# A trunk of four layers: the last down weights ahead of the embedding's, and the experts' outputs scattered as high and low parts

## Chip, cores and metric

The kernel runs on one core of a Trainium2 chip. The metric is the device time of one execution in microseconds, the median of several runs.

## What is computed

Two layers, each an attention and a channel mixer, on 256 tokens of width 1024, all in fp32. The change lies in the second layer's channel mixer, a mixture of experts that picks 2 of 8 for each token, and in the embedding behind it:

```python
def moe_swiglu(x, router_w, router_b, w_gate_up, w_down):
    ...
    for e in range(N_EXPERTS):
        y = y + combine[:, e:e + 1] * swiglu(xf, w_gate_up[e], w_down[e]).astype(F32)
...
    x = layer_norm(DEEPNORM_ALPHA * x + h, ln_ffn_g[i], ln_ffn_b[i])
    x = x + jax.nn.sigmoid(x @ ple_w_gate[i]) * (p[i] @ ple_w_proj[i])
```

An expert's weights are 3 x 1024 x 3584 numbers, 42 MiB; the eight together are 336 MiB.

## The kernel before

**The expert loop.** The experts are taken in turns 0 to 7 (`for e in range(NE)` in `experts`), each with room for 96 or 64 tokens: `GR` counts groups of 32 as (3, 2, 3, 3, 2, 3, 3, 2). `gather` picks an expert's tokens with a matrix of places `pm` (128 tokens x places, ones and zeros) and gives `xg`. An expert has four quarters q. `gate_up(e, q)` multiplies `xg` with gate and up weights, `trans(e, q)` turns the result `h` into `hT`, and `down(e, q)` adds its product with the down weights into `y`. The order in the program is gate_up(e, q), then down(e, q - 1), then trans(e, q); down(e, 3) comes after gate_up(e + 1, 0). Weights are fp32 and move through TensorE 256 columns at a time, four products side by side in strips of 32 columns of the array (`side_by_side`); the trace has two records of each fp32 product.

**The ring.** `ringtile` hands out tiles of 1 MiB in a fixed rotation of 22 (`TURNS`); a tile can be loaded once the one 22 places earlier has been used up. `fetch` takes the weights' tiles, one by one, in the order `items`, on the queue of SyncE; a tile of gate_up in q = 3 comes as two DMAs of 0.5 MiB, and so does the very last tile of down. The embedding's weights and the parts that are made of them take tiles of the same ring, so the order in which `ringtile` is called is also the order of the transfers.

**The scatter.** `y` of an expert stands in PSUM, 32 partitions for each quarter t of the 1024 outputs and 256 columns for each group g: two groups share one bank. `collect` copies it into the SBUF tile `ys`, t = 0, 1 on ACT and t = 2, 3 on DVE. `turn_back` transposes the places, `pm` to `pT`. A product `pT` x `ys` for each half n of the outputs and each block b of 128 tokens puts the rows back to their tokens, and `add` adds it with its gate to the residual `accx`. This hangs on the gate_up(e + 1, 1) of the next expert, as hooks behind its steps k = 0 (turn_back), 2 (first half) and 5 (second half): `SC`.

**The end.** `Finish` holds the second layer's embedding. In turn 7 at q = 3 `finish.load` and `finish.prepare` are called ahead of `down(7, 2)`. `load` brings the projection's weights (1 MiB) and the gate's (4 MiB); `prepare` splits them into an fp32r high part on ACT and the rest, the low part, on DVE (`split`), multiplies p with the projection (24 products), and loads the norm's vectors (1 MiB). `finish.end` is the tail, whose order on each engine is written by hand (`in_order`): collect, place products, adds with statistics, norm, turn into `xT`, products of x with the gate's parts, sigmoid, output. Outside of `in_order` the framework's scheduler fixes each engine's order when the kernel is built: as a rule the order of the program, with later work drawn ahead where it takes earlier work to be waiting.

Of the kernel before, what the change touches and what calls it, by code (L numbers as in the profile page):

```python
# [74 lines left out]
def trunk(ctx: ExitStack, tc: tile.TileContext, cst, x, p, ln_mix_g, ln_mix_b, ln_ffn_g, ln_ffn_b, ab_w_in,  # L75
# [45 lines left out]
    KT = 2  # L121
    SC = (0, 2, 5)
    NLAST = (256, 256)
# [5 lines left out]
    def mis():  # L129
        return psM.tile([P, 512], F32, tag="mis", name="mis")  # L130
# [302 lines left out]
    with pool("hl0", 5, side="right") as hl, ExitStack() as es0:  # L433
# [341 lines left out]
        moe = ctx.enter_context(pool("moe", 1, reuse_waits="tile"))  # L775
        lgT = moe.tile([64, P], F32, tag="pTe", name="lgT", bufs=1)
        V.memset(lgT, 0.0)
        V.memset(lgT[32:33, :], 1.0)
        pm_first = [moe.tile([P, 2 * 3 * CT], F32, tag="pm%d" % b, name="pm", bufs=2) for b in range(NB)]

# [107 lines left out]

    pt1 = moe.tile([P, D], F32, tag="ys", name="pt1", bufs=1)[:, :NB * 256].rearrange("p (b n) -> p b n", b=NB)
    nc.sync.dma_start(pt1, p[1, 0].rearrange("(b p) n -> p b n", p=P))  # L890
# [90 lines left out]
    def experts(rest, finish):  # L981
# [12 lines left out]
        items += [(NE - 1, 3, k) for k in range(chunks[3])]  # L994
        used, passed = [0], [None]

# [23 lines left out]
        def weights(*it):  # L1020
            assert items[used[0]] == it
            used[0] += 1
            return fetch(*it)

# [14 lines left out]
        def gather_first_turn():  # L1039

            xg = xgtile()
            moved = [A.copy(xg[:, k0:k0 + 4, :C0], first[k0 // 4][:, :4 * C0].rearrange("p (k t) -> p k t", t=C0))
                     for k0 in (0, 4)]
            st[0] = dict(xg=xg, pm=[t[:, :C0] for t in pm_first])
            return moved

        def gather(es, src):
# [4 lines left out]
            for b in range(NB):  # L1052
                t = moe.tile([P, 2 * 3 * CT], F32, tag="pm%d" % b, name="pm", bufs=2)
# [99 lines left out]

        def collect(y, ys, n):

            for g in range(n):
                for t in range(4):
                    (A.copy, V.tensor_copy)[t // 2](ys[CT * g:CT * (g + 1), 256 * t:256 * (t + 1)],
                                                    y[g // 2][CT * t:CT * (t + 1), 256 * (g % 2):256 * (g % 2 + 1)])

        def ystile():
            return moe.tile([P, D], F32, tag="ys", name="ys", bufs=1)

        def scatter(e):

            c_ = CT * gr[e]

            def turn_back(after):
                pT = st[e]["pT"] = moe.tile([P, NB, P], F32, tag="pTe", name="pTe", bufs=1)
                ps = mis()  # L1170
                with tc.issue_after(after.ins) if after else nullcontext():
                    for b in range(NB):
                        T.matmul(ps[:c_, b * P:(b + 1) * P], st[e]["pm"][b], ident, start=True, stop=True)
                A.copy(pT[:c_], ps[:c_, :S].rearrange("p (b t) -> p b t", b=NB))

            def half(n):
                def go(after):
                    if n == 0:
                        st[e]["ys"] = ystile()
                        collect(st[e]["y"], st[e]["ys"], gr[e])  # L1180
                    for b in range(NB):
                        po = mis()
                        with tc.issue_after(after.ins):
                            T.matmul(po, st[e]["pT"][:c_, b, :], st[e]["ys"][:c_, 512 * n:512 * (n + 1)],
                                     start=True, stop=True)
                        add(e, b, n, po)
                return go

            return turn_back, half(0), half(1)

# [10 lines left out]
        for e in range(NE):  # L1201
            for q in range(4):
# [16 lines left out]
                trans(e, q)  # L1219
                if e == NE - 1 and q == 3:  # L1220
                    scatter(e)[0](None)
        down(NE - 1, 3)
        ys = ystile()
        finish.end(functools.partial(collect, st[NE - 1]["y"], ys, gr[NE - 1]), ys, st[NE - 1]["pT"], CT * gr[NE - 1],
                   functools.partial(add, NE - 1))

# [6 lines left out]
    class Finish:  # L1233


        def load(self):
            self.pw, self.pTs = ringtile(), ringtile(F32R)
            nc.sync.dma_start(self.pw.rearrange("p (k n) -> p k n", n=D), ple_w_proj[1].rearrange("(k p) n -> p k n", p=P))
            w = ple_w_gate[1].rearrange("(k p) n -> p k n", p=P)
            self.raws = []  # L1240
            for n in range(2):
                for k0 in (0, 4):
                    self.raws.append(ringtile())
                    nc.sync.dma_start(self.raws[-1].rearrange("p (k n) -> p k n", n=512),
                                      w[:, k0:k0 + 4, 512 * n:512 * (n + 1)])

        def parts(self, t, src):
# [3 lines left out]

        def prepare(self):

# [5 lines left out]
            for b in range(NB):  # L1259
                for n in range(2):  # L1260
                    A.copy(self.pp[:, b, half[n]], p_part(([pTs[:, i] for i in range(NB)], pHL), b, n, mis()))
            self.HL = [[], []]
# [5 lines left out]
            self.gb = ringtile()  # L1268
            for i, v in enumerate((ln_ffn_g, ln_ffn_b)):
                nc.sync.dma_start(self.gb[:, D * i:D * (i + 1)], v[1:2, :].broadcast_to([P, D]))  # L1270
# [4 lines left out]
        def end(self, collect, ys, pT, c_, add):  # L1275
# [3 lines left out]
            pos, sgs, done = {}, [], {}  # L1279

            def place(b, n):
                pos[b, n] = acc()
                T.matmul(pos[b, n], pT[:c_, b, :], ys[:c_, half[n]], start=True, stop=True)

# [24 lines left out]
            with in_order():  # L1309
                collect()  # L1310
                for b in range(NB):
                    for n in range(2):
                        place(b, n)
# [69 lines left out]
```

## Time and profile before

| | |
|---|---|
| runs | 1373.24, 1374.14, 1376.18 us; median 1374.14 |
| profiled execution | 1376.53 us, of which the span from first to last instruction is 1374.8 |
| PE busy | 1345.0 us (98%) |
| DVE, ACT busy | 396.1 us (29%), 326.7 us (24%) |
| DMA | 433.77 MB, 316 GB/s over the span |
| expert loop | from 473 to 1331 us |

In what follows a time is counted from the span's first instruction. PE is TensorE, DVE is VectorE, ACT is ScalarE, SP is SyncE, which issues the DMAs. Matmuls are pipelined and the trace models their ends, so neighbouring groups overlap by 0.07 to 0.18 us.

### The profile page before, as it was taken

To read this page: it belongs to the slowest core of one execution; us is meant where nothing else is said; L and a number is where in the kernel's file an instruction comes from. 1 tells how busy PE (TensorE), PEld (TensorE's weight loads), DVE (VectorE), ACT (ScalarE), POOL (GpSimd) and SP (SyncE) were. 2 spreads that over 40 slices of the span, in tenths; PEclk is the share of its full clock that TensorE was granted. 3 is DMA by queue.
4 is the path that set the end of the run, shared out by engine and by line. 5 is a ranking of instruction groups with operands and counts; after the bars stand their busy time and mean duration, and the time that the engine had idled before them with its cause. 6 is when DMAs were issued, how large, how long until landed. Compare 5 with 4: busy or idle time off the path is not lost. (4 is left out here: it accounts for less than half of the span.)

```text
span 1374.8 us, 37450 instructions
## 1 busy us (share of the span) xinstructions
PE 1345.0 (98%) x16967; PEld 891.3 (65%) x16967; DVE 396.1 (29%) x781; ACT 326.7 (24%) x618; POOL 27.5 (2%) x31
## 2 busy tenths in 40 slices
PE   8999999999999999999999999999999999999977
PEld 6786788888776666655556555665555665665546
DVE  5466654555877700010010011001010002002054
ACT  4545444443557100110010010011010001001041
POOL 0000300000000000000000000000000000000000
PEclk9999999999999999999999999999999999999988
DMA  9462564566581899999999999999999999999950
GB/s 323 160 204 74 162 204 138 168 223 198 174 325 68 318 403 405 384 399 400 408 408 401 407 407 392 407 406 392 407 408 395 399 408 406 389 408 407 377 224 34
DMA packets 143146, 433.77 MB, mean 316 GB/s; under 512 B 8834, under 2 KB 14978, under 8 KB 142978
## 3 DMA queue, kind: packets, MB, share of 16 engines
q1 hardware_dynamic: 142834, 431.22, 82.4%
q8 instruction: 135, 2.21, 0.7%
q14 instruction: 33, 0.27, 0.1%
q10 hardware_dynamic: 144, 0.07, 0.0%
HBM read 430.21 MB, written 1.05 MB: 314 GB/s over the span
## 5 line engine op out<-in xcount | busy, mean ns | idle before, releaser
L90 PE MATMUL acc<-raw,xg 128*32 128x256 f32 x9408 | 519.7, 380 | 0.0
L90 PEld LDWEIGHTS acc<-raw,xg 128*32 128x32 f32 x9408 | 300.9, 110 | 209.7 <-issue 11.3
L90 PE MATMUL mis<-raw,hT 128*32 128x256 f32 x4704 | 262.7, 379 | 2.1 <-DMA raw<-in_moe_w_down 2.1
L90 PE MATMUL acc<-H,xT 128*128 128x512 f32 (+2 forms) x768 | 227.8, 380 | 0.8 <-ACT xT L90 0.8
L90 DVE TENSOR_TENSOR h<-h,acc 128x512 f32<-128x512 f32 (+2 forms) x64 | 37.8, 596 | 638.1 <-PE acc L90 478.9
L90 PEld LDWEIGHTS mis<-raw,hT 128*32 128x32 f32 x4704 | 151.8, 110 | 103.7 <-DMA raw<-in_moe_w_down 2.7
L90 DVE TENSOR_TENSOR L<-raw,H 128x1024 fp32r<-128x1024 f32 (+2 forms) x134 | 151.2, 1135 | 110.2 <-ACT H L90 109.6
L90 ACT CAST H<-raw 128x1024 fp32r<-128x1024 f32 (+2 forms) x138 | 133.6, 975 | 147.4 <-PE acc L90 136.9
L90 PEld LDWEIGHTS acc<-H,xT 128*128 128x128 f32 x768 | 141.1, 192 | 29.0 <-ACT xT L90 1.7
L90 ACT ACTIVATE h<-acc 128x512 f32<-128x512 f32 (+2 forms) x64 | 32.9, 522 | 482.8 <-PE acc L90 482.8
L90 PE MATMUL acc<-L,xT 128*128 128x512 f32 (+2 forms) x384 | 141.3, 374 | 0.0
L90 PEld LDWEIGHTS acc<-L,xT 128*128 128x128 f32 x384 | 72.6, 189 | 13.8 <-DVE L L90 1.2
L90 ACT COPY hT<-mis 128x512 f32<-128x512 f32 (+2 forms) x47 | 21.7, 495 | 196.2 <-PE mis L90 195.9
L90 PE MATMUL acc<-H,hT 128*128 128x512 f32 x176 | 55.8, 396 | 0.0
L90 DVE SCALAR_TENSOR_TENSOR x<-mis,gateT,x 128x512 f32<-128x512 f32 x28 | 21.0, 751 | 92.4 <-PE mis L90 90.9
L90 PE MATMUL acc<-H,oT 128*128 128x512 f32 x128 | 43.8, 410 | 0.0
L90 PEld LDWEIGHTS acc<-H,hT 128*128 128x128 f32 x176 | 33.0, 187 | 8.0
L90 PE MATMUL acc<-L,hT 128*128 128x512 f32 x88 | 34.8, 395 | 0.0
L90 DVE COPY ys<-mis 32x256 f32<-32x256 f32 x42 | 17.8, 423 | 48.7 <-ACT ys L90 41.5
L90 PEld LDWEIGHTS mis<-c,h 128*128 128x128 f32 (+1 forms) x212 | 21.7, 140 | 14.0 <-issue 12.3
L90 PE MATMUL mis<-c,h 128*128 128x128 f32 (+1 forms) x212 | 30.1, 271 | 0.0
L90 PEld LDWEIGHTS acc<-H,oT 128*128 128x128 f32 x128 | 23.9, 188 | 7.0 <-issue 1.9
(209 smaller groups left out, 783.7 us busy)
## 6 DMA issues: line engine op xcount, KB each, us to landing
raw<-in_moe_w_gate_up SPq DMA_DIRECT2D x192, 1024.0 KB, 18.2
raw<-in_moe_w_down SPq DMA_DIRECT2D x111, 1024.0 KB, 17.0
raw<-in_moe_w_gate_up SPq DMA_DIRECT2D x64, 512.0 KB, 12.8
raw<-in_ffn_w_gate_up SPq DMA_DIRECT2D x20, 1024.0 KB, 5.2
raw<-in_ffn_w_down SPq DMA_DIRECT2D x10, 1024.0 KB, 5.2
raw<-in_ab_w_in SPq DMA_DIRECT2D x9, 1024.0 KB, 7.7
raw<-in_ple_w_gate SPq DMA_DIRECT2D x8, 1024.0 KB, 13.3
raw<-in_ab_w_out SPq DMA_DIRECT2D x4, 1024.0 KB, 5.2
```

The source lines that it names most:

```text
L90: self.last = getattr(self.eng, name)(*args, **kw)
```

## The change

It has two parts.

**The scatter.** `turn_back` is called in `gather` (and for expert 0 in `gather_first_turn`), as soon as the places exist, so `pm` needs one buffer and `pT` three. `collect` now takes one half n of the outputs and splits each 32x256 piece of y into an fp32r high part (a copy on ACT) and a low part (a subtraction on DVE, which reads the high part). The high part has a buffer for each half, the low part one for both (`ysL0`). A place product becomes two fp32r products, high and low. The hooks move to k = 4 and k = 7.

**The end.** In turn 7 at q = 3 the projection's weights are loaded first, then all down weights that are left, and then the gate's weights and the norm's vectors. The projection is prepared behind `down(7, 2)`, and the splits of the gate's weights stand behind `down(7, 3)` in the program, directly ahead of `finish.end`. In `end` each half is collected and placed for both blocks before the next half.

```diff
-    SC = (0, 2, 5)
+    SC = (4, 7)
...
+        def turn_back(pm, n):
+            pT = moe.tile([P, NB, P], F32R, tag="pTe", name="pTe", bufs=3)
+            ps = mis()
+            for b in range(NB):
+                T.matmul(ps[:n, b * P:(b + 1) * P], pm[b], ident, start=True, stop=True)
+            A.copy(pT[:n], ps[:n, :S].rearrange("p (b t) -> p b t", b=NB))
+            return pT
...
         def gather(es, src):
...
-                st[e] = dict(xg=xg[i], pm=[t[:, o:o + ns[i]] for t in pm])
+                st[e] = dict(xg=xg[i], pT=turn_back([t[:, o:o + ns[i]] for t in pm], ns[i]))
...
+        def collect(y, c_, n):
+            ys = [moe.tile([P, 512], F32R, tag="ys" + "HL"[a] + str(n * (1 - a)), name="ys", bufs=1) for a in range(2)]
+            for g in range(c_ // CT):
+                for t in range(2):
+                    src = y[g // 2][CT * (2 * n + t):CT * (2 * n + t + 1), 256 * (g % 2):256 * (g % 2 + 1)]
+                    split(*(v[CT * g:CT * (g + 1), 256 * t:256 * (t + 1)] for v in ys), src)
+            return ys
...
             def half(n):
                 def go(after):
-                    if n == 0:
-                        st[e]["ys"] = ystile()
-                        collect(st[e]["y"], st[e]["ys"], gr[e])
+                    ys = collect(st[e]["y"], c_, n)
                     for b in range(NB):
                         po = mis()
                         with tc.issue_after(after.ins):
-                            T.matmul(po, st[e]["pT"][:c_, b, :], st[e]["ys"][:c_, 512 * n:512 * (n + 1)],
-                                     start=True, stop=True)
+                            for a in range(2):
+                                T.matmul(po, st[e]["pT"][:c_, b, :], ys[a][:c_], start=(a == 0), stop=(a == 1))
...
                 if e == NE - 1 and q == 3:
+                    finish.load_p()
+                    for it in items[used[0]:]:
+                        got[it] = fetch(*it)
                     finish.load()
-                    finish.prepare()
                 if q:
                     down(e, q - 1)
                 elif e:
                     down(e - 1, 3)
+                if e == NE - 1 and q == 3:
+                    finish.prepare_p()
...
         down(NE - 1, 3)
-        ys = ystile()
+        finish.prepare()
...
             with in_order():
-                collect()
-                for b in range(NB):
-                    for n in range(2):
+                for n in range(2):
+                    ys.append(collect(n))
+                    for b in range(NB):
                         place(b, n)
```

## Rows read from the trace of the kernel before

**Rows 1.** Stretches: span, busy per engine (count), clock, DMA share, GB/s

```profile
600.00:700.00 100.00, 99.09 (x1618) 57.76 (x1614) 8.93 (x16) 10.51 (x27) 2.70 (x4) 1.00 1.03 405
1200.00:1300.00 100.00, 100.00 (x1736) 58.34 (x1730) 8.65 (x15) 8.29 (x18) 0.00 (x0) 1.00 1.02 398
```

**Rows 2.** DMA queues, 640:1280 us in 40 slices: GB/s moved

```profile
GB/s 407 408 408 407 408 401 399 408 409 408 407 408 378 402 408 408 408 402 408 375 406 407 409 406 408 408 362 408 407 409 406 408 407 367 408 407 407 408 408 404
```

**Rows 3.** PE's waits, 600:1300: us in total, times, longest

```profile
PE mis L90 <- ACT xg L90: 0.9, 1, 0.9
```

**Rows 4.** DMA issues in 540:588, then 1010:1030: last column us to landing

```profile
raw<-in_moe_w_gate_up SPq DMA_DIRECT2D x11, 1024.0 KB, 6.7
...
raw<-in_moe_w_gate_up SPq DMA_DIRECT2D x6, 1024.0 KB, 18.6
```

**Rows 5.** Timeline of PE, the scatter of expert 6: start, us, work

```profile
1251.95 0.68 PE L90 MATMUL mis<-c,pm 128*96 128x128 f32 x4
1258.07 5.39 PE L90 MATMUL acc<-raw,xg 128*32 128x256 f32 x96
1263.38 1.98 PE L90 MATMUL mis<-ys,pTe 96*128 96x512 f32 x4
```

**Rows 6.** Last gate-up and last down issue: timeline, then us to landing

```profile
1286.26 0.71 SPq L830 DMA_DIRECT2D raw<-in_moe_w_gate_up  x1
raw<-in_moe_w_gate_up SPq DMA_DIRECT2D x1, 512.0 KB, 10.7
...
1317.73 0.34 SPq L830 DMA_DIRECT2D raw<-in_moe_w_down  x1
raw<-in_moe_w_down SPq DMA_DIRECT2D x1, 512.0 KB, 11.9
```

**Rows 7.** Timelines of PE, ACT and DVE, 1297:1332, some rows

```profile
1297.85 7.09 PE L90 MATMUL acc<-raw,xg 128*32 128x256 f32 x128
1319.35 1.93 PE L90 MATMUL mis<-raw,hT 128*32 128x256 f32 x32 [0.77 <-DMA raw<-in_moe_w_down]
1321.21 0.46 PE L90 MATMUL mis<-c,h 64*128 64x64 f32 x4
1327.19 3.66 PE L90 MATMUL mis<-raw,hT 128*32 128x256 f32 x64 [0.74 <-DMA raw<-in_moe_w_down]
...
1308.94 3.89 ACT L90 CAST raw<-raw 128x1024 fp32r<-128x1024 f32 x4
...
1310.65 8.03 DVE L90 TENSOR_TENSOR raw<-raw 128x1024 fp32r<-128x1024 f32 x7
```

**Rows 8.** Timelines of ACT, DVE and PE behind E

```profile
1330.91 0.74 ACT L90 COPY ys<-mis 32x256 f32<-32x256 f32 x2 [3.96 <-PE mis L90]
1332.57 0.74 ACT L90 COPY ys<-mis 32x256 f32<-32x256 f32 x2 [0.93 <-DVE ys L90]
...
1331.67 0.86 DVE L90 COPY ys<-mis 32x256 f32<-32x256 f32 x2 [12.99 <-ACT ys L90]
1335.47 0.75 DVE L90 SCALAR_TENSOR_TENSOR x<-acc,gateT,x 128x512 f32<-128x512 f32 x1 [1.27 <-PE acc L90]
1337.96 0.69 DVE L90 BATCH_NORM_STATS2 st<-x 128x6 f32<-128x512 f32 x1
...
1342.91 11.09 PE L90 MATMUL acc<-raw 128*128 128x512 f32 x40
1354.64 13.27 PE L90 MATMUL acc<-raw 128*128 128x512 f32 x80
```

**Rows 9.** Stretches of 5 us at the end, for the clock

```profile
1315.00:1320.00 5.00, 4.07 (x51) 2.22 (x53) 3.69 (x4) 2.60 (x4) 0.00 (x0) 1.00 0.94 355
1330.00:1335.00 5.00, 2.49 (x18) 1.14 (x11) 1.69 (x4) 1.45 (x4) 0.00 (x0) 0.79 0.01 3
1340.00:1345.00 5.00, 4.42 (x14) 3.27 (x14) 4.92 (x8) 1.18 (x2) 0.17 (x1) 0.50 0.00 0
1345.00:1350.00 5.00, 5.00 (x20) 4.00 (x20) 3.81 (x8) 0.00 (x0) 0.99 (x1) 0.84 0.00 2
```

More of the change, by code (lines that the diff above doesn't have):

```diff
@@ L775, in trunk @@
         moe = ctx.enter_context(pool("moe", 1, reuse_waits="tile"))
-        lgT = moe.tile([64, P], F32, tag="pTe", name="lgT", bufs=1)
+        lgT = moe.tile([64, P], F32, tag="pTe", name="lgT", bufs=3)
         V.memset(lgT, 0.0)
         V.memset(lgT[32:33, :], 1.0)
-        pm_first = [moe.tile([P, 2 * 3 * CT], F32, tag="pm%d" % b, name="pm", bufs=2) for b in range(NB)]
+        pm_first = [moe.tile([P, 2 * 3 * CT], F32, tag="pm%d" % b, name="pm", bufs=1) for b in range(NB)]
     ring = ctx.enter_context(pool("ring", 1, side="right", reuse_waits="tile"))
@@ L887, in trunk @@
         gather_first(b)
-    pt1 = moe.tile([P, D], F32, tag="ys", name="pt1", bufs=1)[:, :NB * 256].rearrange("p (b n) -> p b n", b=NB)
+    pt1 = moe.tile([P, 512], F32, tag="ysH0", name="pt1", bufs=1)[:, :NB * 256].rearrange("p (b n) -> p b n", b=NB)
     nc.sync.dma_start(pt1, p[1, 0].rearrange("(b p) n -> p b n", p=P))
@@ L1022, in weights @@
             used[0] += 1
-            return fetch(*it)
+            return got.pop(it) if it in got else fetch(*it)
         def place_of(dst, e, b, n):
@@ L1043, in gather_first_turn @@
                      for k0 in (0, 4)]
-            st[0] = dict(xg=xg, pm=[t[:, :C0] for t in pm_first])
+            st[0] = dict(xg=xg, pT=turn_back([t[:, :C0] for t in pm_first], C0))
             return moved
+        def turn_back(pm, n):
[5 more added lines that the diff above has]
+            return pT
         def gather(es, src):
@@ L1052, in gather @@
             for b in range(NB):
-                t = moe.tile([P, 2 * 3 * CT], F32, tag="pm%d" % b, name="pm", bufs=2)
+                t = moe.tile([P, 2 * 3 * CT], F32, tag="pm%d" % b, name="pm", bufs=1)
                 for i, e in enumerate(es):
@@ L1152, in down @@
                     passed[0] = mm
[L1154 to L1162, printed above, removed]
+        def collect(y, c_, n):
[5 more added lines that the diff above has]
+            return ys
         def scatter(e):
             c_ = CT * gr[e]
[L1168 to L1171, printed above, removed]
-                    for b in range(NB):
-                        T.matmul(ps[:c_, b * P:(b + 1) * P], st[e]["pm"][b], ident, start=True, stop=True)
-                A.copy(pT[:c_], ps[:c_, :S].rearrange("p (b t) -> p b t", b=NB))
             def half(n):
                 def go(after):
-                    if n == 0:
-                        st[e]["ys"] = ystile()
-                        collect(st[e]["y"], st[e]["ys"], gr[e])
+                    ys = collect(st[e]["y"], c_, n)
                     for b in range(NB):
@@ L1183, in go @@
                         with tc.issue_after(after.ins):
-                            T.matmul(po, st[e]["pT"][:c_, b, :], st[e]["ys"][:c_, 512 * n:512 * (n + 1)],
-                                     start=True, stop=True)
+                            for a in range(2):
+                                T.matmul(po, st[e]["pT"][:c_, b, :], ys[a][:c_], start=(a == 0), stop=(a == 1))
                         add(e, b, n, po)
                 return go
-            return turn_back, half(0), half(1)
+            return half(0), half(1)
         def add(e, b, n, po):
@@ L1219, in experts @@
                 trans(e, q)
-                if e == NE - 1 and q == 3:
-                    scatter(e)[0](None)
         down(NE - 1, 3)
-        ys = ystile()
-        finish.end(functools.partial(collect, st[NE - 1]["y"], ys, gr[NE - 1]), ys, st[NE - 1]["pT"], CT * gr[NE - 1],
+        finish.prepare()
+        finish.end(functools.partial(collect, st[NE - 1]["y"], CT * gr[NE - 1]), st[NE - 1]["pT"], CT * gr[NE - 1],
                    functools.partial(add, NE - 1))
@@ L1245, in load @@
                                       w[:, k0:k0 + 4, 512 * n:512 * (n + 1)])
+            self.gb = ringtile()
+            for i, v in enumerate((ln_ffn_g, ln_ffn_b)):
+                nc.sync.dma_start(self.gb[:, D * i:D * (i + 1)], v[1:2, :].broadcast_to([P, D]))
         def parts(self, t, src):
@@ L1273, in prepare, with end @@
             self.xT = [ringtile(F32R).rearrange("p (a k t) -> p a k t", a=2, k=8) for b in range(NB)]
-        def end(self, collect, ys, pT, c_, add):
+        def end(self, collect, pT, c_, add):
             x2, xT, HL, pp = self.x2, self.xT, self.HL, self.pp
             do = norm_steps(accx, x2, self.gb[:, :D], self.gb[:, D:], xT)
-            pos, sgs, done = {}, [], {}
+            pos, sgs, done, ys = {}, [], {}, []
             def place(b, n):
                 pos[b, n] = acc()
-                T.matmul(pos[b, n], pT[:c_, b, :], ys[:c_, half[n]], start=True, stop=True)
+                for a in range(2):
+                    T.matmul(pos[b, n], pT[:c_, b, :], ys[n][a][:c_], start=(a == 0), stop=(a == 1))
             def take(b, n):
@@ L1309, in end @@
             with in_order():
-                collect()
-                for b in range(NB):
-                    for n in range(2):
+                for n in range(2):
+                    ys.append(collect(n))
+                    for b in range(NB):
                         place(b, n)
```

11 lines of the change are left out of this document (5 added, 6 removed).

## The prediction, made before the changed kernel was built

> **What bounds the kernel now.** I read the stretches first. From 600 us to about 1300 us TensorE is busy all the time and the DMA queue moves 398 to 405 GB/s [rows 1]; in finer slices it is mostly 407 to 409 GB/s, with a dip now and then, the deepest to 362 [rows 2]. So two resources look full at once. The waits settle which one PE follows: in 700 us it waits once, for 0.9 us, and never for weights [rows 3]. PE runs back to back, behind weights that have already landed. The DMA queue is full all the same: a weight tile lands 18.6 us after its issue around 1010 us, against 6.7 us between 540 and 588 us, where the queue ran short [rows 4]. PE has a reserve of landed tiles, the stream runs at its own ceiling, and the reserve shrinks in the experts with two groups (1.93 us of PE for a tile [rows 7], against 2.57 us of stream for 1 MiB at 408 GB/s). At the end it is nearly spent: the last gate-up half tile is issued at 1286.26 and lands 10.7 us later, at 1297.0 [rows 6], and PE finishes with it at 1304.9 [rows 7]. From there the order of the stream decides. The embedding's weights (1 + 4 MiB) and the norm's vectors (1 MiB) go ahead of the last 6 MiB of down weights, whose last half tile is issued at 1317.73 and lands 11.9 us later, at 1329.6 [rows 6]. PE waits for each down tile, and is done at E = 1330.85 [rows 7]. Everything after E is one chain: copies of y, first place product, two add-and-statistics steps on DVE (done at 1338.65), norm, turn, products from 1342.9 to 1367.9 [rows 8]. The products fill PE, so what counts is when they start.
>
> **The scatter in the expert loop.** A pair of fp32 place products is 4 records and 1.91 us net of the overlap (1.98 - 0.07) [rows 5]. The change makes it 4 fp32r products of 512 columns. The nearest row is the last x80 run: 32 of 512 columns and 48 of 256 in 13.27 us, so 13.27/56 = 0.237 us per 512 [rows 8], 0.95 us for four. Saved: 0.96 us x 14 halves = 13.4 us of PE. Turning the places back costs up to 0.68 us an expert as before [rows 5], only at another place. But PE follows a stream that cannot go faster: the loop's PE gets ahead by up to 13.4 us, uses up the 8 us it is behind (1304.9 - 1297.0), and then waits for weights. Worth at the end of gate-up: 1304.9 to about 1299, and nothing for the stream itself. The doubled copies of y (each 32x256 copy on ACT and a subtraction on DVE) find ACT and DVE busy for only 8 to 11% of the loop [rows 1]. The second half's low part has to wait for the first half's products, since both use one buffer, and then takes up to 6 x 0.85 = 5.1 us (step price below). It has three steps of gate-up to do it in: the three after the first half took 5.39 us with two groups [rows 5], so a stall is 0 to 2 us in three experts, covered by the same reserve.
>
> **A small price early.** Two turn-backs move ahead of 600 us: expert 0's from turn 1, expert 1's from turn 2. Between 540 and 588 us the queue was waiting for PE's releases (6.7 us to landing, [rows 4]), so 2 x 0.68 us of PE there delays the stream, and a full stream never makes it good. Bounds 0 (they fit a gap) to 1.4 us; I take 1.2, as PE shows no gap and expert 1 has fewer places.
>
> **The end of the stream.** 12 MiB land between 1297.0 and 1329.6 in both orders: 32.6/12 = 2.72 us each. Down weights now go after 1 MiB instead of 6: the last lands at 1297.0 + 7 x 2.72 + 1.2 = 1317.2. After it come the four gate tiles at 1319.9, 1322.6, 1325.3, 1328.1, then the two vectors at 1329.4 and 1330.8. Earliest E is 1317.2 + 1.25 (the distance before) = 1318.4. Between 1299 and E PE has six down tiles (11.6 us), 24 embedding products (24 x 0.237 = 5.7 us) and the turn of h (0.46): 17.8 us for 19. It fits if the products lie in the gaps between tiles. The bound on the other side is all of them after the fourth down tile (1311.8 + 1.93): 1313.7 + 5.7 + 0.5 + 3.9 = 1323.8. In the trace other small work, the turn of h at 1321.2, was put between down tiles [rows 7], so I take E = 1319.5: 11.3 us earlier than before.
>
> **What this costs behind E.** Three things, and they nearly eat it. First, collecting y. All of the last expert's y is in one PSUM bank, and ACT and DVE took turns on it (0.74 on ACT, then 0.86 on DVE, then ACT again, each starting as the other ends) [rows 8]. A high part (0.36) and its low part (0.43) make a step of 0.85 us with two hand-overs; eight steps are 6.8 us against 3.3 before, and DVE's first add stands behind all eight in the hand-written order, where before it began with the first place product. Second, the splits of the gate weights. Before, they were done on ACT (0.97 us each) and DVE (8.03/7 = 1.15 us each) by 1318.7, inside the wait for down weights [rows 7]. Now the tiles land from 1319.9 on, so all eight lie behind E, on the engines that collect y: 9.2 us of DVE. Third, in program order the splits come ahead of the collecting, so when both are ready the split goes first. DVE has 9.2 + 3.4 = 12.6 us to do from about 1320. Followed through: the fourth tile lands at 1328.1, its second low part ends at 1328.1 + 2 x 0.97 + 1.15 = 1331.2, by then four of the eight steps are through (one for every tile), and four are left: 1331.2 + 4 x 0.85 = 1334.6. Two adds and statistics, 2 x (0.75 + 0.69) = 2.9 us, end at 1337.5. One wait is new: the low part has one buffer for both halves, so DVE's fifth piece waits for the first half's four products. The lower bound is 0, where a split fills that time; the upper is about 1.5 us, three products behind the fourth piece at half speed (3 x 2 x 0.237 = 1.4) and a hand-over. Nearest is the lower one, since splits are still queued then; I take 0.5, and 1338.0. Before it was 1338.65: 0.65 us gained. The norm's vectors (1330.8) are there by then. What follows is the same work.
>
> **The clock.** The granted clock fell to 0.50, its lower level of 1.2 GHz, in the tail; it is 0.79 in 1330:1335, 0.50 in 1340:1345 and 0.84 in 1345:1350 [rows 9]: 0.84 is two thirds of that stretch at the upper level, so it rose at about 1346.6, some 3.7 us after the products had begun. PE now idles longer ahead of them, and the rise can come earlier or later against that start; 0 to 3 us more at half speed cost 0 to 1.5 us; I take 0.5.
>
> **Sum.** 0.65 - 0.5 = 0.15 us less. The profiled execution took 1376.53 us, of which the span is 1374.8; the median of the three runs is 1374.14, 2.4 us lower. The saving is taken off the median: 1374.0 us. About 0.2% (2.75 us) is what a measurement of this kernel can tell from no change, so this is "the same": some 11 us gained at E, and given back on DVE.
>
> **Rivals.** (1) The collecting goes ahead of the splits. For: ACT and DVE are free at E, and the first gate tile lands only then. Against: the program order. Then 1319.5 + 6.8 + 1.5 + 2.9 = 1330.7 instead of 1338.65, and some low parts still stand in the way: 4 to 8 us faster, 1368. Chance 0.1. (2) The collecting overlaps within the bank. The trace shows turns being taken, so I keep the step at 0.85. The Trainium skill, "PSUM — Partial Sum Buffer" (PSUM bank collisions raise a hardware error), says that two engines may use one bank together as long as they are in different 32-partition quadrants, and the pieces of y are in different ones; this trace does not agree as programmed, since DVE's copy of quadrant 2 begins only when ACT's of quadrant 1 ends. If the steps overlapped, each would cost 0.43, four left would be 1.7 instead of 3.4, and more would be done earlier: 2 to 4 us faster, 1371. Chance 0.1. (3) Slower: all eight splits are queued ahead of the collecting on both engines, which take their work in order. Then nothing is collected until 1331.2: + 6.8 + 1.5 + 2.9 = 1342.4, that is 3.8 us later than before, and with 0 to 1.5 of the clock 4 to 5 us slower: 1378.5. It decides from the point where six or more low parts precede DVE's first piece of y. For: the program order, and all splits stand ahead of the copies in the trace of before [rows 7, 8]. Against: there they had landed long before. Also here: E at 1323.8 with the splits first. Chance 0.22. (4) The stream is not at its ceiling and gains from PE's earlier releases: up to 7 us faster; the flat 408 GB/s speaks against it. Chance 0.03. (5) PE now waits for every tile of the last 40 us. The Trainium skill, "TensorE: Matmul & The Clock Gate" (HAM oscillation), says that a kernel that waits for DMA between short bursts is throttled again and again. In the trace waits of 0.7 to 0.8 us for down tiles [rows 7] left the clock at 1.00 in 1315:1320 [rows 9], so I give this no chance of its own. At the lower level a tile would take up to 3.86 us instead of 1.93 and E would come later by up to 6 x 1.1 = 7 us, which ends like (3).
>
> **How the numbers follow.** The likeliest case, near no change, has 0.55, at 1372 to 1377 by itself (the bounds of E, of the one buffer and of the clock). Faster by over 0.2%: rivals 1 and 4, most of 2 and an edge of the likeliest, 0.25. Slower: rival 3, 0.22. Within: 0.53. The range takes in rival 3 and rival 1 up to its middle: 1368 to 1378.5.
>
> **What would show it.** Right: pairs of place products in the loop near 1 us instead of 1.98; PE waiting for weights from about 1275 us; E near 1319.5; the splits of the gate weights between E and 1332 with pieces of y between them on DVE; statistics done near 1338. Wrong: y collected in one run of 7 us right behind E, or the weight stream ending more than 2 us off 1330.8, or E beyond 1324.

## The result, and the profile after

The changed kernel takes 1385.24 us (median of four runs, 1383.75 to 1386.38) against 1374.56 for the kernel before beside it (1373.24 to 1376.18): ratio 1.0077, 95% interval 1.0059 to 1.0094. It is 10.7 us slower, and outside the forecast range. The profiled execution took 1385.69 us, of which the span is 1383.9.

| us from the span's start | before | forecast | after |
|---|---|---|---|
| PE done with gate-up | 1304.9 | 1299 | 1298.9 |
| last down weights landed | 1329.6 | 1317.2 | 1316.9 |
| norm's vectors landed | | 1330.8 | 1330.0 |
| E, y complete | 1330.85 | 1319.5 | 1338.15 |
| statistics of block 0 done | 1338.65 | 1338.0 | 1349.23 |
| products with x begin | 1342.91 | | 1353.50 |

The stream came as forecast. The issue of the last down tile, then of the second vector, and what each took to land (a line's DMA issues with first and last start; DMA issues, last column us to landing; timeline of SP's queue), kernel after:

```profile
L830 SPq DMA_DIRECT2D raw<-in_moe_w_down x7: 373/613/2269, 1289.9 to 1300.1; - x7
raw<-in_moe_w_down SPq DMA_DIRECT2D x1, 512.0 KB, 16.8
...
1317.03 2.66 SPq L1250 DMA_DIRECT2D raw<-in_ln_ffn_b  x1
raw<-in_ln_ffn_b SPq DMA_DIRECT2D x1, 512.0 KB, 13.0
```

1300.1 + 16.8 = 1316.9 and 1317.03 + 13.0 = 1330.0. E did not come as forecast. The timeline of PE after (start, us, work, the idle time before it and what ended it), which answers to [rows 7, 8]:

```profile
1297.84 1.07 PE L90 MATMUL acc<-raw,xg 128*32 128x256 f32 x16 [0.29 <-DMA raw<-in_moe_w_gate_up]
1303.35 7.07 PE L90 MATMUL mis<-raw,hT 128*32 128x256 f32 x96 [4.43 <-DMA raw<-in_moe_w_down]
1310.93 1.93 PE L90 MATMUL mis<-raw,hT 128*32 128x256 f32 x32 [0.51 <-DMA raw<-in_moe_w_down]
1324.72 8.82 PE L90 MATMUL mis<-raw 128*128 128x512 f32 x24 [11.86 <-ACT raw L90]
1334.49 3.66 PE L90 MATMUL mis<-raw,hT 128*32 128x256 f32 x64 [0.56 <-ACT hT L90]
1341.16 2.10 PE L90 MATMUL acc<-ys,pTe 64*128 64x512 f32 x4 [3.01 <-ACT ys L90]
1353.50 10.19 PE L90 MATMUL acc<-raw 128*128 128x512 f32 x40
```

PE follows the down tiles until 1312.86 and then stands 11.86 us. What it waits for is ACT's, ahead of the 24 products of p with the projection. All down weights lie there from 1316.9 on, but the products with the last 2 MiB (x64) stand behind p's in PE's order, and E is 1334.49 + 3.66. The timelines of ACT and DVE say what ACT was doing, and what follows E:

```profile
1300.46 1.99 ACT L90 CAST raw<-raw 128x1024 fp32r<-128x1024 f32 x2 [0.89 <-DMA raw<-in_ple_w_proj]
1319.67 1.99 ACT L90 CAST raw<-raw 128x1024 fp32r<-128x1024 f32 x2 [17.22 <-DMA raw<-in_ple_w_gate]
1322.37 1.99 ACT L90 CAST raw<-raw 128x1024 fp32r<-128x1024 f32 x2 [0.71 <-DMA raw<-in_ple_w_gate]
1324.27 0.71 ACT L90 CAST raw<-pT 128x256 fp32r<-128x256 f32 x2
...
1332.01 1.23 DVE L90 TENSOR_TENSOR raw<-raw 128x1024 fp32r<-128x1024 f32 x1 [0.91 <-ACT raw L90]
1338.61 0.41 DVE L90 TENSOR_TENSOR ys<-mis,ys 32x256 fp32r<-32x256 f32 x1 [5.37 <-ACT ys L90]
1339.45 0.42 DVE L90 TENSOR_TENSOR ys<-mis,ys 32x256 fp32r<-32x256 f32 x1 [0.43 <-ACT ys L90]
1343.36 0.42 DVE L90 TENSOR_TENSOR ys<-mis,ys 32x256 fp32r<-32x256 f32 x1 [1.80 <-PE acc L90]
1348.54 0.69 DVE L90 BATCH_NORM_STATS2 st<-x 128x6 f32<-128x512 f32 x1
```

The split of p's turned parts (`raw<-pT`, 0.71 us; its input is from turn 0) stands in ACT's order behind four casts of gate weights. These wait 17.22 us for their first tile, which the new order of the loads sends behind all down weights. So a transfer that was put behind the down weights holds the last down products all the same, through one short instruction of ACT. Behind E y is collected in steps of 0.84 us with one wait of 1.80 for the single low buffer, and the statistics are done 11.08 us after E, 7.80 before.

The loss thus lies in two places: E + 7.30 us and E to statistics + 3.28, with - 0.90 for the first 40 products (10.19 us for 11.09 in [rows 8]). That is 9.7 us, against 9.1 between the spans of the two profiled executions and 10.7 between the medians.

### The profile page after: what moved, and what is told of

Its sections match the earlier page's. It is cut to its first block, busy times and chain, and to the rows that moved or that the text cites. A ratio compares the mean times of both kernels' runs of the same rounds, so it can differ in the third digit from the quotient of the medians.

```text
span 1383.9 us, 37528 instructions
## 1 busy us (share of the span) xinstructions
PE 1336.7 (97%) x16967; PEld 891.1 (64%) x16967; DVE 411.9 (30%) x823; ACT 342.1 (25%) x660; POOL 27.4 (2%) x31
## 5 line engine op out<-in xcount | busy, mean ns | idle before, releaser
L90 PE MATMUL mis<-raw,hT 128*32 128x256 f32 x4704 | 267.7, 381 | 5.5 <-DMA raw<-in_moe_w_down 4.9
L90 ACT CAST ys<-mis 32x256 fp32r<-32x256 f32 x84 | 30.5, 363 | 123.6 <-DVE ys L90 87.1
L90 DVE TENSOR_TENSOR ys<-mis,ys 32x256 fp32r<-32x256 f32 x84 | 35.3, 420 | 52.0 <-ACT ys L90 48.8
## 6 DMA issues: line engine op xcount, KB each, us to landing
raw<-in_moe_w_down SPq DMA_DIRECT2D x111, 1024.0 KB, 18.1
```

Source lines behind the costliest of these rows:

```text
L90: self.last = getattr(self.eng, name)(*args, **kw)
```

## The experiments

All times are medians beside runs of the kernel before (1374.0 to 1374.4); E, statistics and products are from each profiled execution. That one execution can lie 2 to 3 us off the median (order alone 1378.85 for 1380.82, loop alone 1378.60 for 1375.25, slot 1379.81 for 1377.57, two banks 1374.01 for 1371.38), so its columns say where the time goes, and only roughly how much.

| run | time | ratio, interval | E | statistics | products |
|---|---|---|---|---|---|
| other slot for p's parts | 1377.57 | 1.0024, 1.0014 to 1.0033 | 1323.53 | 1341.58 | 1345.84 |
| gate splits forced behind p's | 1382.48 | 1.0061, 1.0047 to 1.0074 | 1333.68 | 1344.77 | 1349.04 |
| scatter alone | 1378.81 | 1.0038, 1.0024 to 1.0052 | 1330.77 | 1341.85 | 1346.11 |
| load order alone | 1380.82 | 1.0052, 1.0039 to 1.0066 | 1333.91 | 1340.45 | 1344.71 |
| scatter in the loop alone | 1375.25 | 1.0008, 0.9999 to 1.0018 | 1332.98 | 1340.78 | 1345.04 |
| load order, slot, hand order | 1372.39 | 0.9987, 0.9977 to 0.9996 | 1326.28 | 1334.72 | 1339.04 |
| change, slot, hand order | 1373.22 | 0.9992, 0.9982 to 1.0001 | 1323.21 | 1336.59 | 1340.91 |
| the same, last y whole in fp32 | 1369.28 | 0.9964, 0.9951 to 0.9976 | 1321.07 | 1332.11 | 1336.43 |
| change, slot, hand order, two banks | 1371.38 | 0.9983, 0.9973 to 0.9992 | 1323.18 | 1335.41 | 1339.72 |
| p's products around the collecting | 1371.63 | 0.9982, 0.9972 to 0.9991 | 1318.60 | 1327.41 | 1333.84 |
| the same, low parts on DVE | 1370.04 | 0.9969, 0.9958 to 0.9981 | 1320.61 | 1329.42 | 1334.18 |
| the same, and two banks | 1368.50 | 0.9957, 0.9941 to 0.9974 | 1320.79 | 1328.92 | 1332.87 |

**Another slot for p's parts.** In the rotation of the ring, p's parts and the projection's weights change places; nothing else:

```diff
-            self.pw, self.pTs = ringtile(), ringtile(F32R)
+            self.pTs, self.pw = ringtile(F32R), ringtile()
```

> One line: the buffers of the projection's weights and of p's parts change places, so that p's parts get a ring tile of their own instead of one of the seven that circulate. My theory: E is late (1338.15) because ACT's order has p's split behind four gate splits that wait for gate weights, and PE's order has the last two down tiles behind the products of p; the only cause is that no buffer was free for p's parts when the order was fixed. Then E falls from 1338.15 to 1319 to 1321, the products of p lie between the down tiles, and the time is near that of the kernel before, 1372 to 1377 us. Rival A: the new order of the loads costs this by itself, whichever buffer p's parts have: E stays beyond 1330 and the time at 1382 to 1386. Rival B: the dearer collecting and the splits behind E are the loss: E falls, but the time stays above 1380.

1377.57, 7.7 us under the change: the 11.86 us are gone. PE and ACT in this run:

```profile
1302.10 3.35 PE L90 MATMUL mis<-raw 128*128 128x512 f32 x7 [3.74 <-ACT raw L90]
1305.38 3.21 PE L90 MATMUL mis<-raw,hT 128*32 128x256 f32 x32
1308.53 1.65 PE L90 MATMUL mis<-raw 128*128 128x512 f32 x6
1319.87 3.66 PE L90 MATMUL mis<-raw,hT 128*32 128x256 f32 x64 [0.56 <-ACT hT L90]
...
1325.66 1.99 ACT L90 CAST raw<-raw 128x1024 fp32r<-128x1024 f32 x2
1327.68 0.36 ACT L90 CAST ys<-mis 32x256 fp32r<-32x256 f32 x1
1328.07 2.00 ACT L90 CAST raw<-raw 128x1024 fp32r<-128x1024 f32 x2
```

Now p's products lie between the down tiles (7, 6, 5, 5, 1), as the prediction had it. E is 1323.53, not 1319 to 1321, and the time 0.6 us above the expected range: PE idles 3.74 us until the projection is split, and seven products and a down tile then run at the lower clock (3.21 us for a tile that takes 1.93). Behind E the gate casts alternate with the pieces of y, and the statistics come 18.05 us after E.

**Gate splits forced behind p's.** The slot is left as in the change, and every gate split is ordered behind p's on both engines:

```diff
...
-                H, L = self.parts(ringtile(F32R), self.raws[i // 2][...])
+                H, L = self.parts(ringtile(F32R), self.raws[i // 2][...], self.turned_p)
...
```

> The changed kernel with one constraint of order: the first gate splits on ACT and DVE stand behind p's split. Buffers and everything else stay. Theory: p's products run right behind the fourth down tile (about 1313), E is 1322 to 1324, but all eight gate splits still stand ahead of the collecting, so this is the slower rival of the prediction: low parts end near 1331.5, statistics at 1331.5 + 8.1 + 2.9 = 1342.5 against 1338.65 of the kernel before and 1349.3 of the changed one, and the time is 1377 to 1380. Rival A: E beyond 1330 and 1382 to 1386.

A miss: 1382.48. p's split came at 1302.86, but its products were held one step later, by the same queue:

```profile
1302.86 0.71 ACT L90 CAST raw<-pT 128x256 fp32r<-128x256 f32 x2
1320.10 1.99 ACT L90 CAST raw<-raw 128x1024 fp32r<-128x1024 f32 x2 [16.54 <-DMA raw<-in_ple_w_gate]
1322.78 1.99 ACT L90 CAST raw<-raw 128x1024 fp32r<-128x1024 f32 x2 [0.68 <-DMA raw<-in_ple_w_gate]
1324.67 0.58 ACT L90 COPY raw<-mis 128x512 f32<-128x512 f32 x1
...
1325.30 2.93 PE L90 MATMUL mis<-raw 128*128 128x512 f32 x6 [7.75 <-ACT raw L90]
```

The copies that empty p's PSUM tiles (`raw<-mis`) stand behind the same four casts; PE fills three tiles, waits 7.75 us for room and then goes on. It is not the one instruction that matters, but that anything PE needs stands behind a cast that waits for late weights. E and the time lie where rival A had put them, but not for its reason: with the other slot the same load order has E at 1323.53.

**Each part alone.** Scatter alone keeps the load order of before:

```diff
                     finish.load_p()
-                    for it in items[used[0]:]:
-                        got[it] = fetch(*it)
                     finish.load()
+                    finish.prepare_p()
+                    finish.prepare()
...
```

> The scatter's part alone: the loads and the preparing in the order of the kernel before, the high and low parts and the earlier turn-back kept. Theory: PE ends gate-up of the last quarter near 1299 instead of 1305 and gains nothing, since the stream of weights ends at about 1330.4 (0.8 later, by the turn-backs moved early); E is near 1331.7; the tail pays 11.1 us from E to the statistics against 7.8. The sum is +3.3 + 0.8 = 4 us: 1378 to 1380. Rival B says more, 1383 to 1386. If the saved PE time counted, it would be 1362 to 1370.

Load order alone is the kernel before with the loads of the change: the lines marked - above are in it and those marked + are not, and p's projection and the gate splits stand where the change puts them. Scatter and slots are those of before.

> The order of the loads and of the preparing alone, with the scatter and the buffers of the kernel before. Theory: p's split stands behind gate splits here too, so E is 1336 to 1338 as in the changed kernel, while the tail from E is that of before (7.8 us to the statistics): 1374.6 + 6 to 7 = 1380 to 1382. Rival B: E about 1320 and a time at or below 1374.

Both times are as expected: 1378.81 and 1380.82, 0.38% and 0.52%, together 0.90% against 0.77% (0.59 to 0.94) for the whole. With the scatter alone E is that of before (1330.77 for 1330.85), and all is lost behind it (E + 11.08). With the order alone E is late, by less than expected (1333.91, not 1336 to 1338):

```profile
1303.27 7.12 PE L90 MATMUL mis<-raw,hT 128*32 128x256 f32 x128
1321.41 7.90 PE L90 MATMUL mis<-raw 128*128 128x512 f32 x24 [11.02 <-ACT raw L90]
1330.25 3.66 PE L90 MATMUL mis<-raw,hT 128*32 128x256 f32 x64
```

This execution does not account for the whole loss. From E to the statistics it took 6.54 us and not 7.80, since its eight place products ran in 3.73 us (clock 1.00 in 1335:1340) for 7.19 before, so the products begin 1.80 us later than before and the span is 2.3 us longer, where the medians are 6.4 apart. Its time, 1378.85, was the lowest of five; where the others lost more is not shown.

**The scatter in the loop alone.** As scatter alone, but the last expert's y is collected as before, in two fp32 copies on each engine and one place product a half (`collect_whole`), with the old load order.

> The scatter of the change in the expert loop alone: the loads keep the order of the kernel before, and the last expert's y is collected whole in fp32 (two copies on ACT, two on DVE, one fp32 place product a half) as before. The run with all of the scatter change but the old load order took 4.4 us more than the kernel before, and its trace puts 3.3 us of it between E and the statistics (E+11.08 against E+7.80). Theory (the split of y behind E is the whole price of the scatter): E at 1330.5 to 1331, statistics at E+7.5 to E+8.2, products at 1342 to 1344, time 1374 to 1376. Rival (the scatter also costs in the loop or in the early stream, by the turn-backs moved ahead): E at 1332 or later, time 1377 to 1379. Second rival (the loop's saved PE time is worth something in the stream): E before 1329, time under 1373.

1375.25: the loss of the scatter is the split behind E, and in the loop the saved PE time is worth nothing that can be measured. E was 2 us late in the profiled execution (gate-up ended at 1300.66), whose 1378.60 was the highest of ten times; the median does not show that, and why it was late is open.

**With the gate splits put by hand.** In the next three, p's parts have the other slot, and the splits stand in the hand-written order: those of the first half ahead of the collecting, those of the second behind block 0's low parts.

```diff
             with in_order():
+                for i in range(4):
+                    self.gate(i)
...
                 for n in range(2):
                     do.x_low(0, n)
+                for i in range(4, 8):
+                    self.gate(i)
...
```

First with the load order alone, the scatter as before:

> The load order of the change alone (scatter as before), with p's parts in a slot of their own and the gate splits put by hand into the order of the tail: the four of the first half ahead of the collecting of y, the four of the second half behind the low parts of block 0's norm. Theory (what costs is only where the engines' fixed orders put work that waits for a late tile; with that mended the earlier down weights are worth what the stream gives): p's products lie between the down tiles, E at 1320 to 1323.5, first-half splits done by 1324, statistics at 1330 to 1332, products at 1334 to 1337, time 1366 to 1369. Rival (the four low parts put into DVE's chain of block 1 hold its turn up, and PE waits between the x40 run and the rest): products start as early, PE waits 2 to 5 us ahead of block 1's products, time 1369 to 1373. Second rival (the clock: PE idles about 12 us ahead of the products and runs at half speed well into them): x40 run 11 us or more, time 1370 to 1372.

1372.39, 3 to 6 us more than expected, and not for either rival's reason: E was 1326.28. Without the loop's scatter PE ends gate-up at 1303.75 (1296.66 + 7.09), and from 1306.65 to E it has no gap:

```profile
1296.66 7.09 PE L90 MATMUL acc<-raw,xg 128*32 128x256 f32 x128
1305.39 0.96 PE L90 MATMUL mis<-raw 128*128 128x512 f32 x3 [1.65 <-ACT raw L90]
1306.65 1.60 PE L90 MATMUL mis<-raw 128*128 128x512 f32 x4 [0.30 <-DVE raw L90]
1322.62 3.66 PE L90 MATMUL mis<-raw,hT 128*32 128x256 f32 x64
```

Then the whole change:

> The whole change, with p's parts in the other slot (as in the run that moved only the slot: E at 1323.5, statistics at E+18.05, 1377.6) and the gate splits put by hand: first half ahead of the collecting, second half behind the low parts of block 0's norm. Theory (in the slot run it was the eight splits between the pieces of y that held the statistics up): E at 1323 to 1324, y collected in one run of 7 to 8.2 us, statistics at E+10.5 to E+12 (1334 to 1336), products at 1338 to 1340, time 1369 to 1373. Rival (the split pieces of y behind E cost by themselves and the order of the gate splits does not matter): statistics at 1340 or later, time 1376 to 1378.

1373.22, and 4.4 us under the run with the slot alone. The statistics come at E + 13.38 instead of 18.05; 1.4 us more than expected, since collecting waits for the second pair of casts (to 1324.5) and its low parts (to 1325.9). And with the last expert's y whole:

> As the run above, and the last expert's y collected whole in fp32 as in the kernel before (two copies on ACT, two on DVE), with the scatter of the change kept in the loop. Theory (the split costs 3.3 us behind E, since the pieces go one after another through one PSUM bank): E at 1323 to 1324, statistics at E+7.5 to E+8.5 (1331 to 1332.5), products at 1335 to 1337, time 1366 to 1369, that is 3 to 4 us under the run above. Rival (with the split gone something else is late next, above all the norm's vectors, which landed at 1328.2 and 1329.4 in the slot run, or the second half's gate parts): statistics early but the norm or the products wait, time 1369 to 1372.

1369.28, 3.9 us less than the split, and faster than the kernel before by 0.36%. Of the 4.5 us at the statistics 0.7 is that collecting began sooner (1323.69 for 1324.39); the rest goes with the split. But the statistics come at E + 11.04, not E + 7.5 to 8.5: as the rival had it, something else is late next, the gate tiles of the first half, ahead of the collecting:

```profile
1319.08 1.99 ACT L90 CAST raw<-raw 128x1024 fp32r<-128x1024 f32 x2 [1.72 <-DMA raw<-in_ple_w_gate]
1321.79 1.99 ACT L90 CAST raw<-raw 128x1024 fp32r<-128x1024 f32 x2 [0.72 <-DMA raw<-in_ple_w_gate]
...
1317.41 3.66 PE L90 MATMUL mis<-raw,hT 128*32 128x256 f32 x64 [0.56 <-ACT hT L90]
1326.82 7.19 PE L90 MATMUL acc<-ys,pTe 64*128 64x512 f32 x8 [5.75 <-ACT ys L90]
1336.43 10.31 PE L90 MATMUL acc<-raw 128*128 128x512 f32 x40
```

**Two banks.** In the run of the whole change by hand, the last expert's two groups get a PSUM bank each, and the pieces alternate:

```diff
-            for g in range(c_ // CT):
-                for t in range(2):
-                    src = y[g // 2][...]
+            for t in range(2):
+                for g in range(c_ // CT):
+                    src = y[g][0][...]
...
```

> As the run of the whole change with the other slot and the gate splits by hand (1373.2, statistics at E+13.4; y collected from 1324.39 to 1333.71 in eight steps of 0.84 and one wait of 1.81), but the last expert's two groups of y lie in two PSUM banks and the pieces alternate between them. Theory (ACT and DVE take turns because both read one bank): ACT's cast runs beside DVE's low part, DVE's pieces follow each other in about 0.42 to 0.5, the wait for the one low buffer stays, y is collected 2 to 3.5 us sooner, time 1369.5 to 1371.5. Rival (turns are taken for another reason, such as the dependence of a low part on its high part alone): steps of 0.84 as before, time 1372.5 to 1374.

As expected, 1371.38. DVE's eight low parts:

```profile
1327.19 1.75 DVE L90 TENSOR_TENSOR ys<-mis,ys 32x256 fp32r<-32x256 f32 x4
1330.73 1.78 DVE L90 TENSOR_TENSOR ys<-mis,ys 32x256 fp32r<-32x256 f32 x4 [1.79 <-PE acc L90]
```

Four follow each other in 1.75 us, 0.44 each where it was 0.84; the wait for the one low buffer stays. y is collected in 6.9 us instead of 9.3. It began 1.2 us later than in the run without (1325.62 for 1324.39), so the statistics come only 1.2 us sooner. The order of the pieces changed too, but the change's own trace speaks for the bank: in its loop the experts with two groups, all in one bank, are collected in steps of 0.84, while five low parts of an expert with three groups, in two banks, follow each other in 2.24 us (DVE from 1255.68).

**p's products around the collecting.** From the fastest run so far: p's products go ahead of and behind the place products, y is collected ahead of the gate splits, the vectors are loaded ahead of the gate's second half, and the second half's low parts go to POOL.

```diff
+                ps = {n: p_part(self.prep, 0, n, mis()) for n in range(2)}
                 ys.extend(collect())
...
+                for i in range(4, 8):
+                    self.gate_low(i, G)
```

> As the fastest run so far (1369.28: E at 1321.07, products at 1336.43), with p's products taken from between the down tiles and put half ahead of and half behind the place products of the last expert, y collected ahead of the gate splits, the norm's vectors loaded ahead of the second half's gate weights, and the second half's low parts on POOL. Theory (E is held by p's 5.8 us of PE in front of it, and PE idles behind E): E at 1317 to 1318.5, statistics at 1326 to 1328, products at 1331 to 1334, the clock is up again sooner as PE idles less, time 1363 to 1367. Rival (POOL's subtractions, 2.6 us each in the trace of before, come too late or slow DVE down): PE waits 2 to 6 us for low parts behind the start of the products, time 1367 to 1370. Second rival (fewer idle gaps do not matter, since DVE's chain with two gate low parts more in it sets the start): products at 1335 or later, time 1368 to 1370.

1371.63, a miss (1363 to 1367), and no better than the run it came from (1369.28; the two intervals just overlap): products began 2.6 us sooner and the gain was given back. The timelines of PE, DVE and POOL:

```profile
1333.84 8.61 PE L90 MATMUL acc<-raw 128*128 128x512 f32 x36 [0.29 <-ACT raw L90]
1345.66 0.83 PE L90 MATMUL acc<-raw 128*128 128x512 f32 x2 [1.58 <-POOL raw L90]
...
1337.10 3.96 DVE L90 SCALAR_TENSOR_TENSOR raw<-x,mv,raw 128x512 f32<-128x512 f32 x2
1346.15 1.42 DVE L90 SCALAR_TENSOR_TENSOR raw<-raw,rs 128x512 f32<-128x512 f32 x2 [5.08 <-POOL rs L90]
...
1335.30 10.31 POOL L90 TENSOR_TENSOR raw<-raw 128x1024 fp32r<-128x1024 f32 x4 [6.34 <-ACT raw L90]
```

PE waits for POOL's low parts, DVE's norm step of block 1 takes 3.96 us, and DVE then waits 5.08 for `rs`, which stands behind the low parts on POOL. With them on DVE (`self.gate_low(i, V)` behind block 1's statistics):

> As the run with p's products around the collecting (1371.6; there products began at 1333.84, PE then waited 2.5 us for POOL's low parts, DVE's first norm step of block 1 took 3.96 us instead of 1.40 beside POOL, and block 1's turn came at 1346.96), with the second half's four low parts on DVE behind block 1's statistics instead of on POOL. Theory (POOL's four subtractions are what gave the gain back): products at 1333 to 1335, no wait for POOL, block 1's turn at 1344 to 1346, time 1366 to 1369. Rival (DVE's 4.6 us of low parts hold block 1 up as long as POOL did): block 1's turn at 1347 or later, time 1370 to 1372.

1370.04: the waits for POOL are gone and block 1 is turned at 1345.63 instead of 1346.96, although E is 2.0 us later, so POOL was what held it. The time is 1 us more than expected, though products and block 1's turn came when they should: PE runs the last 80 products in 14.33 us, at a clock of 0.66 in 1345:1350, where the next run takes 13.24 at 1.00. E gained little too: 1320.61, only 0.5 sooner than with p's products between the down tiles.

```profile
1303.32 6.19 PE L90 MATMUL mis<-raw,hT 128*32 128x256 f32 x64 [4.48 <-DMA raw<-in_moe_w_down]
1305.00:1310.00 5.00, 5.00 (x57) 2.79 (x50) 0.00 (x0) 0.00 (x0) 0.00 (x0) 0.65 1.02 406
```

The second row is a stretch (columns as in [rows 1]): a clock of 0.65. Two tiles take 6.19 us for 3.66, behind 4.48 us in which PE had no work. At last two banks for the fp32 copies as well:

> As the run above, with the last expert's two groups of y in two PSUM banks, so that ACT's and DVE's fp32 copies run side by side. Theory (one bank makes them take turns): y collected in about 1.7 us instead of 3.3, statistics and products 1 to 1.6 us sooner than in the run above, time 0.5 to 1.5 us under it. Rival (DVE waits for the first half's gate tiles anyway, which land at about 1318.5 and 1321): the start moves by less than 0.5 us, time within 0.5 us of the run above.

1368.50, the fastest: 1.54 us under the run above (the two intervals overlap), 0.43% under the kernel before. p's last 12 products in the run above, then here:

```profile
1327.96 5.06 PE L90 MATMUL mis<-raw 128*128 128x512 f32 x12
1326.25 3.02 PE L90 MATMUL mis<-raw 128*128 128x512 f32 x12
```

The statistics are only 0.5 us sooner, since DVE's first gate low part waits 1.04 us for ACT's cast. Most of the rest comes with the clock: PE stood 1.17 us ahead of the place products instead of 2.52, the clock in 1325:1330 was 1.00 and not 0.55, the products with x began 1.31 us sooner, and the last 80 took 1.1 us less.

## Why the prediction was wrong, step by step

**The bound, the stream, the loop: right.** PE ended gate-up and the last down weights landed within 0.3 us of the forecast, and the loop's saving alone brought nothing (1375.25). PE first waited for weights at 1294.89, though, and not from about 1275. The saving itself was put at 13.4 us; it was 10.9. A pair after, then groups of the loop's place products by shape, of before, then of after (count, then busy us and mean ns):

```profile
1253.47 1.20 PE L90 MATMUL mis<-ys,pTe 96*128 96x512 f32 x4
```

```profile
L90 PE MATMUL mis<-ys,pTe 96*128 96x512 f32 x40 | 19.8, 618 | 0.0
L90 PE MATMUL mis<-ys,pTe 64*128 64x512 f32 x16 | 7.9, 615 | 0.0
```

```profile
L90 PE MATMUL mis<-ys,pTe 96*128 96x512 f32 x40 | 12.0, 421 | 0.0
L90 PE MATMUL mis<-ys,pTe 64*128 64x512 f32 x16 | 4.8, 418 | 0.0
```

27.7 - 16.8 = 10.9. A product of 512 columns in a run of four costs some 0.28 us (1.20 less 0.07 of overlap, over four), not the 0.237 of a run of 80. That nothing hung on it holds for the old load order only: with the new one and the slot put right, PE and not the stream sets E, and the three runs by hand with the loop's scatter have E between 1321.07 and 1323.21, the one without at 1326.28.

**The early price (1.2 us): open.** The last gate-up tile lands 0.8 us later than before (1297.8 for 1297.0), but from run to run it lands between 1295.6 and 1299.5. The three profiled executions with the scatter of before have 1295.6 to 1297.0, the eleven with that of the change 1296.6 to 1299.5, on average 1.6 us later; that speaks for a price of this size, but no run has the early turn-backs alone.

**E: the step that failed.** The prediction let p's 24 products "lie in the gaps between tiles", with a bound of 1323.8 for all of them behind the fourth tile. Both ends counted PE's time and the down tiles alone. A product needs its operands too: p's parts had to be split on ACT, and the prediction never asked where that split stands in ACT's order and what stands ahead of it. It stood behind four casts that wait for the very tiles that the change makes late. Taking the wait and the half-clocked products out of the measured E gives 1338.15 - 11.86 - (8.82 - 5.7) = 1323.2, close to the prediction's upper bound of 1323.8, and the run with the other slot has 1323.53. There p's products were mis-sized too: in five short runs, the first at the lower clock, they took some 8.3 us and not 5.7. The Trainium skill, "PSUM — Partial Sum Buffer" (Engine vs sequencer instructions), says that ScalarE's and VectorE's queues are strictly first in, first out; the trace agrees in both forms, as the split that waits (after) and as the copy out of PSUM that waits (splits forced). That the slot of the ring decides the place of p's split is shown by the swap; by which rule the builder placed it there is not.

**Behind E.** Steps of 0.85 were right (0.84). The wait for the one low buffer was taken at 0.5 with a bound of 1.5; it costs 1.80 - 0.43 = 1.4, close to the bound, because no gate split was left to fill it. Splits ahead of the collecting cost nothing here: they ended at 1333.24, before E. In the run with the other slot they do lie between the pieces of y, and E to statistics is 18.05 us where the prediction has 18.5 (1319.5 to 1338.0). That the two agree so well is partly luck. DVE's work was sized right (9.4 us of splits and 3.4 of pieces, for 9.2 and 3.4). But the prediction let it hang on the landing of the fourth gate tile, with the last low part at 1331.2 and four pieces behind it. In the run every split stands behind the third piece of y, though the first tile had landed by 1319.9 (issued at 1301.81, at most 18.1 us to landing); DVE's splits run from 1326.74 to 1337.38, and two pieces come behind them.

**The clock.** A loss of 0.5 us at the first 40 products was forecast; they took 0.9 us less than before. What the clock cost lay ahead of E, in p's products (8.82 us), which rival (5) had named and priced for down tiles, without a chance.

**The rivals.** (3), all splits queued ahead of the collecting, met its condition, but not its mechanism: the delay was ahead of E, on ACT and not DVE. Its size, 4 to 5 us, is half of what came. (1), collecting before the splits, was tried with the last y in fp32 and brings E to statistics down to 8.8 us. (2), overlap within one bank, did not happen; across two banks it did: the medians are 1.5 and 1.8 us lower with it, with overlapping intervals, the products with x begin 1.2 to 1.3 us sooner, and part of that is the clock.

## What to carry to other kernels

When loads are put in another order, list every instruction that waits for a load that became later, on each engine that takes its work in order, and then everything that stands behind it: a cast of 1 us whose weights come 17 us later stops a split of 0.7 us, and through it the matrix engine. Bounding a stage by the time of its matmuls is not enough; walk each operand back to the engine that makes it. And put work that waits for late loads into the order by hand, where its place among the rest is yours to choose.

## What the runs showed of the hardware

- POOL holds up DVE, but only some of its work. While POOL subtracted (2.4 to 2.8 us each) DVE's norm step with both operands in SBUF took 3.96 us a pair, and 1.41 in the run with the low parts on DVE; an add that reads PSUM took 0.74 in both. The Trainium skill, "SBUF — State Buffer" (two separate sides), says that an instruction of DVE with two SBUF inputs and one of POOL that reads SBUF lock each other out for a whole instruction; these rows agree.
- ACT and DVE read one PSUM bank in turns as the kernel is built, 0.84 us a step, and two banks side by side, 0.44.
- PE's clock: after 4.48 us without work two down tiles took 6.19 us (clock 0.65 in 1305:1310). The length of the wait alone does not tell what follows: with the last y whole in fp32 p's products came after 2.61 us and the clock stayed at 1.00 from 1300 to 1315; with the whole change in two banks they came after 2.62 us and it was 0.80 in 1300:1305 and 0.86 in 1305:1310; with the load order by hand they came after 1.65 us and it was 0.72 in 1305:1310, where a tile took 3.13 us for 1.93. What decides it is not shown.
